# Result rows of two token tiles summed and normed among the experts, in the order of the tokens' groups

## The chip, the cores and the metric

One core of one Trainium2 chip runs the whole kernel. The metric is the time of one execution on the chip in microseconds (us), the median of several. The core's engines work side by side, each through its own list of instructions in order: TensorE (PE, matrix products), VectorE (DVE) and ScalarE (ACT, element-wise work and evictions), GpSimd (POOL), and SyncE (SP), which here only issues transfers. Transfers (DMA) are issued by SP, by ACT or by POOL and run on 16 DMA engines. An instruction that waits for a semaphore holds what stands behind it on its engine.

## The reference

One layer on 512 tokens of width 1024, in float32: attention in two branches (stick-breaking, and chunked with relative positions), gates, an output projection, a layer norm; then experts and a second layer norm. The experts are what the change is about:

```
g_sel = argmax over 4 groups of  x @ w_group + b_group            # one group per token
e     = the two best of the group's 8 experts, softmax over the two
y     = sum over the two: weight * (silu(x @ gate_e) * (x @ up_e)) @ down_e
x     = layer_norm(ALPHA * x + y) * ln2_g + ln2_b                 # x: result of the first norm
```

There are 32 experts, 1024 -> 256 -> 1024, and each token goes to two experts of one group. In the inputs used here the four groups hold 123, 132, 127 and 130 tokens, and no expert has more than 44.

## The kernel before

Up to about 400 us come the projections, the attention, the gates and the output projection, each fp32 product in three passes of split operands (`xh`, `xl`, `wh`, `wl`). Keys are evicted from a product (`pj`) in halves of 64 rows, each half written twice: into its own rows (L334, L336) and into the other head's rows (L335, L337).

Then the tokens are routed. Each expert has 64 slots, two experts are a pair, and 16 pairs make up the 32 experts. Routing leaves for every slot its token (`toki`), its weight (`wslot`) and the row that it writes (`rowi`, in `y2D`: two rows for each token, one for each of its experts). If an expert should have over 64 tokens, a flag sends all work through `dense`, behind the rest.

Each expert e runs: `gate_up(e)` (16 products `sc` of the pair's gathered rows `xp` with four weight tiles), the eviction of its two halves (`gus`: ScalarE at L1105, VectorE's add at L1106), `down(e-1)` (8 products `tr` with two weight tiles, evicted to `oe` by ScalarE and VectorE), the transposes and activation `act(e)` (`stp`, L1113, `sg`). Every other expert prepares the next pair: GpSimd gathers its rows (`fetch`, `xg`), TensorE turns them (`pj`, L1082), ScalarE and VectorE evict `xp`. After an odd expert GpSimd scatters the pair's results into `y2D` (L1147).

A weight tile `we` is 512 KB, 192 of them; SyncE loads them in the order of use (L1029: load 6e-2 to 6e+1 are gate and up of expert e from the second on, 6e+8 and 6e+9 its down part), up to 47 ahead, into four rings of buffers. At expert 20 it also loads the tokens' rows `hb` (L1299), at expert 28 the result rows `yy` (L1173), two loads for each of the four tiles of 128 tokens. The scheduler that lays out each engine's list keeps what the code pins in order, and puts transfers where it expects their buffers free.

The last two pairs (`NLATE = 2`) write no rows: their results (`late`, split in two) are added through a product with a one-hot matrix `stl`. So all four tiles are finished behind the last expert, from a list of steps (`FIN`): for each tile, products of `hb`, `yy` and `late` are collected in `fin`, then statistics, mean and gain (L1236 to L1262), and the rows go out by a plain transfer.

Of the kernel before, what the change touches and what calls it, by code (L numbers as in the profile page):

```python
# [18 lines left out]
P = 128  # L19
# [43 lines left out]
HB_AT = 20  # L63
# [12 lines left out]
Y_PE = (3,)  # L76
Y_POOL = (0, 1, 2)
F_DVE = (3,)
G_ACT = ()
FIN_TAG = ("pj", "pj", "tr", "sc", "sc", "av", "tr", "tr")  # L80
FIN_AT = {29: (0, 1, 2, 3)}
FIN = (
# [6 lines left out]
).split()  # L89
# [10 lines left out]
def trunk(ctx, tc, xT, x, wm, wv, wbr, wout, wr, br, bg, rbx, lnp, lncol, wexp, out):  # L100
# [36 lines left out]
    hD = dram.tile([S, D], F32, name="hD")  # L137

# [115 lines left out]
    ps = pp.tile([P, S], F32, tag="sc", name="warm", bufs=SCB)  # L254
    for _ in range(WARM):
        nc.tensor.matmul(ps, warm[:, :P], warm, start=True, stop=True)
# [48 lines left out]
    def proj(m_hl, evac):  # L305
        h, lo = m_hl
        ps = pp.tile([P, S], F32, tag="pj", name="pj", bufs=2)
        for c in range(C):
            mm3(ps, h[:, c * P : (c + 1) * P], lo[:, c * P : (c + 1) * P], xh[c], xl[c], c == 0, c == C - 1)
            if c % 2 == 1:  # L310
                if c == C - 1:
                    evac(ps)
                yield

    def job(kind, *a):
        if kind in ("q", "k"):
# [5 lines left out]
            def evac(ps):  # L322
                in_order[0] = (b, p) == (0, 0)

                for h in range(2):
# [14 lines left out]
            yield from proj(hl, evac)  # L340
# [230 lines left out]
    while first:  # L571
        first = [g for g in first if next(g, True) is not True]
# [73 lines left out]
    val = small([P, TT, 2], "val", at=end0)  # L646
    tokv = small([P, TT, 2], "tokv", at=end0)
# [46 lines left out]
    tok2 = keep.tile([P, 2 * NLATE], F32, name="tok2")  # L694
    flag = keep.tile([P, 1], I32, name="flag")
    xg = [keep.tile([P, D], F32, name=f"xg{k}") for k in range(XGB)]
    for t in xg:
        nc.gpsimd.memset(t, 0.0)
    onehot = keep.tile([P, TT, 4 * CAP], F32R, name="onehot")
    nc.gpsimd.memset(ones, 1.0)  # L700
# [4 lines left out]
    iota([P, TT, 2], [[2 * P, TT], [1, 2]], -2 * S, 2, "val", val)  # L705
# [145 lines left out]
    def route(tt):  # L851
# [7 lines left out]
        m = small([P, 4], f"m{tt}")  # L859
# [20 lines left out]
        mm(rk, tri, MS[:, tt, :], False, True)  # L880
        pm = small([P, 2, NE], f"pm{tt}")
# [12 lines left out]
    def finish_routing():  # L894
# [10 lines left out]

        pmf = B8[:, :2].rearrange("p q t k n -> p (q t k n)").rearrange("p (k t e) -> p k t e", k=2, t=TT)
# [20 lines left out]

        for k in range(2):
            for j in range(2):
                nc.scalar.activation(  # L930
                    tok2[j * HD : (j + 1) * HD, k * NLATE : (k + 1) * NLATE],
                    ps[k * HD : (k + 1) * HD, 1, NPAIR - NLATE :], AF.Copy, bias=1.0 * S,
                )
        nc.scalar.activation(wslot, ps[:, 2, :], AF.Copy)
# [82 lines left out]
    for e in range(NE + 1):  # L1017
        seq += [(e, c) for c in range(4) if e < NE] + [(e - 1, 4 + f) for f in range(2) if e > 0]
# [74 lines left out]
    def gate_up(e):  # L1093
# [11 lines left out]
        nc.scalar.activation(gus[e], ps[CAP:], AF.Copy)  # L1105
        nc.vector.tensor_add(gus[e], gus[e], ps[:CAP])  # L1106
# [3 lines left out]
    def act(e):  # L1110
# [41 lines left out]
    res, fs, fr, fu, parts = {}, {}, {}, {}, {}  # L1152
    stl = []
    gb2 = []
    late = []

    def last_rows():

        tok3 = bp.tile([P, 2 * NLATE], F32, tag="tok3", name="tok3", bufs=1)
        nc.vector.tensor_scalar(out=tok3, in0=tok2, scalar1=-256.0, scalar2=None, op0=OP.add)  # L1160
        for n in range(NLATE):
            st = lop.tile([P, 2, 2, 256], F32R, tag="lo", name=f"stl{n}")
            for k in range(2):
# [257 lines left out]
```

## Time and profile before

| | us |
|---|---|
| median of 3 runs (691.07 to 693.62) | 691.54 |
| the profiled execution | 692.49 |
| its span, first to last instruction | 690.8 |
| TensorE busy | 646.1 |
| VectorE, ScalarE, GpSimd busy | 400.8, 322.0, 86.9 |

The profile is of one execution, 0.95 us over the median, and 1.7 us of its time lie outside the span. Times inside it count from the span's start. "Busy" is time in which an engine has an instruction at work; a matrix product that waits for nothing still counts its pipeline. The stage table gives the busy time of each engine in one stretch; the chain of waits follows the span back from its last instruction, step by step to what released it; the timeline lists instructions in order of time, and merges neighbours of one kind (x16).

### The profile page before, as it was taken

The page shows a single profiled execution, that of the slowest core. Times are in us where ns is not written, and L with a number is a line of the kernel's source. Part 1 is how long each engine was busy: PE and PEld are TensorE (multiplying, and loading weights), DVE is VectorE, ACT ScalarE, POOL GpSimd, SP SyncE. Part 2 cuts the span into 40 slices and gives each one's busy share as a digit, 9 for nine tenths or more (in the row PEclk, how much of TensorE's full clock was granted, in tenths as well). Part 3 has the DMA queues.
Part 4 walks back from the last instruction along what each step waited for, and adds up shares of the span by engine and source line. Part 5 has one row for each costly group of instructions (what it writes and reads, how often), then busy time and mean ns, then how long its engine had stood idle before and what let it go on. Part 6 is the DMA issues. An engine that isn't in the chain of part 4 may idle for free.

```text
span 690.8 us, 8854 instructions
## 1 busy us (share of the span) xinstructions
PE 646.1 (94%) x3096; PEld 419.8 (61%) x3096; DVE 400.8 (58%) x834; ACT 322.0 (47%) x632; POOL 86.9 (13%) x134
## 2 busy tenths in 40 slices
PE   8999999899999999989999978999999988899992
PEld 4888788788878888878888764343433322223351
DVE  6776867768868887563864895233323322224347
ACT  5677877866765665745423222222322222223232
POOL 2001100101000000050000232211111111000043
PEclk9999999999999999999999999999999999999997
DMA  9600078102130322027793489999999999999923
GB/s 332 247 0 1 1 279 297 65 0 93 46 106 17 115 82 94 31 64 261 262 381 129 168 283 391 407 411 409 409 410 407 408 405 411 405 405 407 408 103 123
DMA packets 48319, 160.15 MB, mean 232 GB/s; under 512 B 7438, under 2 KB 7582, under 8 KB 48272
## 3 DMA queue, kind: packets, MB, share of 16 engines
q1 hardware_dynamic: 44208, 152.26, 57.9%
q0 software_dynamic: 4064, 7.31, 2.8%
q8 instruction: 25, 0.41, 0.2%
q14 instruction: 22, 0.18, 0.1%
HBM read 151.20 MB, written 15.73 MB: 242 GB/s over the span
## 4 chain that ended last, share of the span: by engine, by line
PE 67%; DMA 14%; DVE 12%; ACT 4%; issue 3%; SPq 0%; DVEq 0%; ACTq 0%
PE pj L126 22%; PE sc L126 13%; DMA we<-in_wexp_dram 13%; PE pv L126 6%; PE pb L126 6%; PE tr L126 6%; PE po L126 4%; PE av L126 2%; PE fin L126 2%; PE tr L523 2%; PE pj L1082 1%; DVE hp L809 1%; PE stp L1113 1%; DVE wl L111 1%; ACT wh L108 1%
## 5 line engine op out<-in xcount | busy, mean ns | idle before, releaser
L126 PE MATMUL sc<-we,xp 128*64 128x512 f32 x448 | 108.4, 604 | 3.9 <-DMA we<-in_wexp_dram 2.9
L126 PE MATMUL pj<-xh,wh 128*128 128x512 f32 x256 | 103.5, 406 | 2.4 <-DVE k L337 1.6
L126 PE MATMUL pj<-xh,wl 128*128 128x512 f32 x256 | 101.5, 396 | 0.5 <-DVE wl L111 0.5
L126 PE MATMUL pj<-xl,wh 128*128 128x512 f32 x256 | 101.5, 396 | 0.2 <-DVE xl L111 0.2
L111 DVE TENSOR_TENSOR wl<-raw,wh 128x1024 fp32r<-128x1024 f32 (+1 forms) x57 | 68.3, 1204 | 19.9 <-ACT wh L108 19.7
L1106 DVE TENSOR_TENSOR gus<-gus,sc 64x512 f32<-64x512 f32 x32 | 21.7, 679 | 97.0 <-ACT gus L1105 97.0
L126 PE MATMUL tr<-we,sg 128*64 128x512 f32 x256 | 65.0, 615 | 8.1 <-DMA we<-in_wexp_dram 6.0
L1105 ACT ACTIVATE gus<-sc 64x512 f32<-64x512 f32 x32 | 19.0, 594 | 108.5 <-PE sc L126 108.5
L108 ACT ACTIVATE wh<-raw 128x1024 fp32r<-128x1024 f32 (+1 forms) x57 | 58.7, 1038 | 19.8 <-PE pj L126 5.2
L126 PEld LDWEIGHTS sc<-we,xp 128*64 128x64 f32 x448 | 27.2, 136 | 60.2 <-issue 27.5
L126 PEld LDWEIGHTS pj<-xh,wh 128*128 128x128 f32 x256 | 49.1, 192 | 13.1 <-ACT wh L108 2.0
L126 PEld LDWEIGHTS pj<-xh,wl 128*128 128x128 f32 x256 | 48.7, 190 | 12.0 <-DVE wl L111 1.4
L126 PEld LDWEIGHTS pj<-xl,wh 128*128 128x128 f32 x256 | 49.0, 191 | 8.9 <-DVE xl L111 0.5
L126 PEld LDWEIGHTS tr<-we,sg 128*64 128x64 f32 x256 | 16.7, 138 | 49.4 <-issue 33.0
L126 PE MATMUL pb<-y,wh 128*128 128x512 f32 x128 | 40.0, 394 | 1.9 <-DVE k L337 1.9
L111 DVE TENSOR_TENSOR wl<-tr,wh 128x512 fp32r<-128x512 f32 (+1 forms) x64 | 30.7, 484 | 9.9 <-ACT wh L108 9.6
L476 POOL TENSOR_SCALAR_AFFINE_SELECT w<-w 128x128 f32<-128x128 f32 x32 | 14.6, 467 | 148.8 <-ACT w L473 146.1
L108 ACT ACTIVATE wh<-tr 128x512 fp32r<-128x512 f32 (+1 forms) x64 | 27.5, 431 | 12.0 <-PE tr L523 11.0
L126 PE MATMUL sc<-k,q 128*128 128x512 f32 (+3 forms) x128 | 29.3, 324 | 0.9 <-DVE w L472 0.9
L1147 POOL DMA_INDIRECT y2D<-oe,rowi x14 | 14.1, 1007 | 120.9 <-DVE oe L1145 93.3
L126 PEld LDWEIGHTS pb<-y,wh 128*128 128x128 f32 x128 | 23.3, 188 | 7.0 <-PE tr L523 1.6
L523 PE MATMUL tr<-ident,w 128*128 128x128 f32 x160 | 27.5, 272 | 0.0
(222 smaller groups left out, 1181.4 us busy)
## 6 DMA issues: line engine op xcount, KB each, us to landing
we<-in_wexp_dram SPq DMA_DIRECT2D x192, 512.0 KB
raw<-in_wm_dram SPq DMA_DIRECT2D x32, 512.0 KB
raw<-in_wv_dram SPq DMA_DIRECT2D x8, 512.0 KB
y2D<-zero SPq DMA_DIRECT2D x16, 256.0 KB
raw<-in_wbr_dram SPq DMA_DIRECT2D x8, 512.0 KB
raw<-in_wout_dram SPq DMA_DIRECT2D x8, 512.0 KB
yy<-y2D SPq DMA_DIRECT2D x8, 512.0 KB
strip<-in_rbx_dram SPq DMA_DIRECT2D x8, 256.0 KB
```

The costliest lines, as they stand in the source:

```text
L108: act = nc.scalar.activation(hi, src, AF.Copy)
L111: pin((eng or nc.vector).tensor_sub(lo, src, hi.bitcast(F32)), fix == "both")
L126: pin(nc.tensor.matmul(ps, a, b, start=start, stop=stop))
L476: nc.gpsimd.affine_select(out=blk, in_=blk, pattern=[[-1, P]], compare_op=OP.is_gt, fill=0.0, base=0, channel_multiplier=1)
L523: nc.tensor.transpose(tr[:, i * P : (i + 1) * P], w[:, off + j * P : off + (j + 1) * P], ident)
L809: nc.vector.scalar_tensor_tensor(out=src, in0=src, scalar=r, in1=lnb[:, cs], op0=OP.mult, op1=OP.add)
L1082: pin(nc.tensor.transpose(ps[:, c, :], xg[(p - 2) % XGB][:, o : o + P], ident))
L1105: nc.scalar.activation(gus[e], ps[CAP:], AF.Copy)
L1106: nc.vector.tensor_add(gus[e], gus[e], ps[:CAP])
L1113: pin(nc.tensor.transpose(st[:, q, :], gus[e][:, q * P : (q + 1) * P], ident[:CAP, :CAP]))
L1147: nc.gpsimd.indirect_dma_start(out=y2D[:, :], out_offset=bass.IndirectOffsetOnAxis(ap=rowi[:, p : p + 1], axis=0), in_=oe[p], in_offset=No ...
```

## The change

Tokens are given positions in the order of their groups (four counts `cg`, starts `sp`, a token's place `posi`), and `y2D` is written by position. Tile 0, the first 128 positions, has all its rows after the experts of the first two groups, tile 1 after those of the third, if these groups hold at least 128 and 256 tokens; if not, the flag of `dense` is set as well. Tiles 0 and 1 are summed and normed on VectorE at experts 24 and 29, tiles 2 and 3 behind the last expert. Tokens' own rows come by an indirect gather (`tokp`, which passes through a small table `tokD` in memory), the finished rows leave by an indirect scatter. The y loads move from SyncE to ScalarE. Expert 29's down part is computed one place later. Apart from that, 14 of the 16 copies of keys go to GpSimd, and products whose result is not used are put between products at the start and in the routing.

```diff
-HB_AT = 20
+BETWEEN = (3, 3, 1, 1)
+IDLE = {(1, 4, 4): 6, (1, 4, 5): 12}
+IDLE_LAST = 6
+K_POOL = ((0, 1), (0, 2), (0, 3), (1, 0), (1, 1), (1, 2), (1, 3))
+ROWS_AT = {22: 0, 27: 1}
+NORM_AT = {24: 0, 29: 1}
+GAIN_AT = 21
+TOKP_AT = 8
...
                         pin(nc.scalar.activation(t[r, h, 0, :], ps[r], AF.Copy))
-                        pin(nc.scalar.activation(t[o, h, 0, :], ps[r], AF.Copy))
                         pin(nc.vector.tensor_sub(t[r, h, 1, :], ps[r], t[r, h, 0, :].bitcast(F32)))
-                        pin(nc.vector.tensor_sub(t[o, h, 1, :], ps[r], t[r, h, 0, :].bitcast(F32)))
+                        if (b, p) in K_POOL:
+                            nc.gpsimd.tensor_copy(t[o, h, :, :], t[r, h, :, :])
...
+        V.tensor_scalar(out=posi, in0=p2[:, 0], scalar1=0.5, scalar2=1.0 * S, op0=OP.mult, op1=OP.add)
...
+    seq += [(e, 4 + f) for e in range(NE - 3, NE) for f in range(2)]
...
-        for tt in range(TT):
-            y2.append([slot([P, D], F32, f"yy{tt}{k}") for k in range(2)])
-            for k in range(2):
-                nc.sync.dma_start(y2[tt][k], y2v[tt, k])
...
+    def tile_rows(tt, pool):
+        for y, k, where in ((ya, 0, pool), (yb, 1, slots2)):
+            y[tt] = slot([P, D], F32, f"y{k}{tt}", where)
+            nc.scalar.dma_start(y[tt], y2v[tt, k])
+
+    def tile_res(tt):
+        hb[tt] = slot([P, D], F32, f"hb{tt}", slots2)
+        nc.gpsimd.indirect_dma_start(
+            out=hb[tt], out_offset=None, in_=hD[:, :],
+            in_offset=bass.IndirectOffsetOnAxis(ap=tokp[:, tt : tt + 1], axis=0),
+            bounds_check=S - 1, oob_is_err=False,
+        )
+
+    def tile_sum(tt, eng):
+        pin(eng.tensor_add(ya[tt], ya[tt], hb[tt]))
+        pin(eng.tensor_add(ya[tt], ya[tt], yb[tt]))
+
+    def tile_norm(tt, src, out_by):
+...
+        nc.gpsimd.indirect_dma_start(
+            out=out[:, :], out_offset=bass.IndirectOffsetOnAxis(ap=tokp[:, tt : tt + 1], axis=0),
+            in_=ya[tt], in_offset=None, bounds_check=S - 1, oob_is_err=False,
+        )
...
+        if e == NE - 1:
+            down(e - 2)
+        elif 0 < e < NE - 2:
             down(e - 1)
...
+        if e in ROWS_AT:
+            tile_res(ROWS_AT[e])
+            tile_rows(ROWS_AT[e], slots2)
+        if e in NORM_AT:
+            t = NORM_AT[e]
+            tile_sum(t, nc.vector)
+            tile_norm(t, (ya[t][:, :S], ya[t][:, S:]), "vector")
...
+    tile_sum(2, nc.vector)
+    tile_sum(3, nc.gpsimd)
...
+    tile_norm(2, fin[:2], "both")
+    tile_norm(3, fin[2:], "vector")
```

What this makes of the engines' lists shows in three places. Names in brackets are the semaphores that an instruction waits for: DMAHW0 to 7 are those of transfers issued by SP and ACT, DMASW of those by GpSimd. The first place is ScalarE at expert 23. Before, the eviction gus of expert 23 comes first, then the last part of expert 22's results and the rows of pair 12:

```order
L1105 ACTIVATE gus<-sc 64x512 [waits DVE_49,PE_49]
L1143 ACTIVATE oe<-tr,wslot 64x512 [waits DMASW6_49,PE_49,Activation_49]
L1061 ACTIVATE xp_5284<-pj 128x512 [waits PE_49]
L1115 ACTIVATE sg<-stp 128x128 [waits PE_49]
L1105 ACTIVATE gus<-sc 64x512 [waits DVE_49,PE_49]
```

The last of these rows is gus of expert 24. After the change, the list at the same place is this:

```order
L1201 ACTIVATE oe<-tr,wslot 64x512 [waits DMASW2_49,PE_49,Activation_49]
L1117 ACTIVATE xp_5409<-pj 128x512 [waits PE_49]
L1244 DMA y_5373<-y2D 128x1024 [waits DMAHW3_49,DMAHW1_49,DMAHW5_49,DMAHW0_49,DMASW4_49]
L1244 DMA y_5375<-y2D 128x1024 [waits DMAHW6_49,DMAHW4_49,DMAHW1_49]
L1164 ACTIVATE gus<-sc 64x512 [waits DVE_49]
L1174 ACTIVATE sg<-stp 128x128 [waits PE_49]
```

The last row but one is now gus of expert 23: it has moved behind oe and xp, and two transfers of result rows stand ahead of it, which wait for DMAHW5 and DMAHW6 among others.

The second place is SyncE at the loads that had these semaphores last. Before, the list is weights, then the four hb, then weights again:

```order
L1029 DMA we_5117<-in_wexp_dram 128x1024 [waits DMAHW1_49,PE_49]
L1029 DMA we_5125<-in_wexp_dram 128x1024 [waits DMAHW2_49,PE_49]
L1029 DMA we_5129<-in_wexp_dram 128x1024 [waits DMAHW3_49,PE_49]
L1299 DMA hb_5146<-hD 128x1024 [waits DMAHW4_49]
L1299 DMA hb_5148<-hD 128x1024 [waits DMAHW5_49]
L1299 DMA hb_5150<-hD 128x1024 [waits DMAHW6_49]
L1299 DMA hb_5152<-hD 128x1024 [waits DMAHW7_49]
L1029 DMA we_5155<-in_wexp_dram 128x1024 [waits DMAHW0_49]
```

After the change, the two loads number 162 and 163 (we_5137, we_5141) come first here, and the order of use is left five rows further:

```order
L1083 DMA we_5137<-in_wexp_dram 128x1024 [waits DMAHW5_49]
L1083 DMA we_5141<-in_wexp_dram 128x1024 [waits DMAHW6_49,PE_49]
L1083 DMA we_5172<-in_wexp_dram 128x1024 [waits DMAHW7_49,PE_49]
L1083 DMA we_5176<-in_wexp_dram 128x1024 [waits DMAHW0_49,PE_49]
L1083 DMA we_5180<-in_wexp_dram 128x1024 [waits DMAHW1_49]
L1083 DMA we_5214<-in_wexp_dram 128x1024 [waits DMAHW2_49]
L1083 DMA we_5235<-in_wexp_dram 128x1024 [waits DMAHW3_49]
L1083 DMA we_5336<-in_wexp_dram 128x1024 [waits DMAHW4_49]
L1083 DMA we_5378<-in_wexp_dram 128x1024 [waits DMAHW7_49,PE_49]
L1083 DMA we_5399<-in_wexp_dram 128x1024 [waits DMAHW0_49,PE_49]
```

The hb loads are gone from the queue, and six weights of later experts (we_5214 is number 170, we_5442 number 190) stand ahead of number 167.

The third place is ScalarE from expert 28 to 30. Before, the two splits of expert 28's `late` stand ahead of gus of expert 30, those of expert 29 ahead of gus of expert 31:

```order
L113 ACTIVATE late_5586<-tr,wslot 64x512 [waits DMAHW1_49,PE_49]
L1061 ACTIVATE xp_5596<-pj 128x512 [waits PE_49]
L113 ACTIVATE late_5586<-tr,wswap 64x512 [waits DVE_49]
L1115 ACTIVATE sg<-stp 128x128 [waits PE_49]
L1105 ACTIVATE gus<-sc 64x512 [waits PE_49]
L113 ACTIVATE late_5641<-tr,wswap 64x512 [waits DMAHW7_49,DMAHW2_49,PE_49]
L1115 ACTIVATE sg<-stp 128x128 [waits PE_49]
L113 ACTIVATE late_5641<-tr,wslot 64x512 [waits DVE_49]
L1105 ACTIVATE gus<-sc 64x512 [waits PE_49]
```

After the change, from gus of expert 29 to gus of expert 30, the loads of tiles 2 and 3 stand there, and the norm of tile 1:

```order
L1164 ACTIVATE gus<-sc 64x512 [waits DVE_49,PE_49]
L1244 DMA y_5721<-y2D 128x1024 [waits DMAHW7_49,DMAHW0_49,DMASW5_49]
L110 ACTIVATE late_5670<-tr,wslot 64x512 [waits PE_49]
L1117 ACTIVATE xp_5680<-pj 128x512 [waits PE_49]
L1174 ACTIVATE sg<-stp 128x128 [waits PE_49]
L1244 DMA y_5723<-y2D 128x1024 [waits DMAHW0_49,DMASW1_49]
L110 ACTIVATE late_5670<-tr,wswap 64x512 [waits DVE_49]
L1244 DMA y_5725<-y2D 128x1024 [waits DMAHW2_49,DMAHW1_49]
L1244 DMA y_5727<-y2D 128x1024 [waits DMAHW2_49]
L1268 ACT_TABLE_LOAD
L1268 ACTIVATE mv<-mv,epsf 128x1 [waits DVE_49]
L1164 ACTIVATE gus<-sc 64x512 [waits PE_49]
```

Four transfers, a table load and the norm's logarithm now stand ahead of gus of expert 30.

## Rows read from the trace of the kernel before

**Rows 1.** Stage table: stretch, length, busy PE, PEld, DVE, ACT, POOL, clock

```profile
421.00:536.00 115.00, 111.64 (x567) 42.35 (x566) 36.41 (x69) 32.24 (x67) 18.29 (x18) 0.99 1.03 409
...
536.00:655.00 119.00, 107.49 (x488) 35.43 (x486) 35.09 (x73) 28.69 (x55) 10.07 (x10) 1.00 1.02 407
```

**Rows 2.** Chain of waits, experts: start us, us, what

```profile
450.38 3.58 PE sc L126 x16
...
462.79 3.58 PE sc L126 x16
...
536.13 12.01 DMA we<-in_wexp_dram
...
649.96 0.39 PE stp L1113 x4
```

**Rows 3.** Timeline of SyncE's queue: start us, us, what, count

```profile
611.40 4.12 SPq L1299 DMA_DIRECT2D hb<-hD  x4
...
617.85 27.72 SPq L1029 DMA_DIRECT2D we<-in_wexp_dram  x22
```

**Rows 4.** Waits of SyncE's queue: us in total, times, longest

```profile
SPq L1029 <- DMA we<-in_wexp_dram: 152.5, 146, 2.3
```

**Rows 5.** Timeline of the end, all engines

```profile
657.86 1.28 ACT L1117 ACT_TABLE_LOAD   x1
...
658.83 1.94 PE L126 MATMUL tr<-we,sg 128*64 128x512 f32 x8 [1.49 <-DVE sg L1119]
...
663.02 0.75 DVE L114 SCALAR_TENSOR_TENSOR late<-tr,wslot,late 64x512 fp32r<-64x512 f32 x1 [0.75 <-ACT late L113]
...
673.23 5.31 PE L126 MATMUL fin<-yy,ident 128*128 128x512 f32 x12
...
675.85 0.69 DVE L1236 BATCH_NORM_STATS2 bsf<-fin 128x6 f32<-128x512 f32 x1
...
677.50 0.75 DVE L1254 SCALAR_TENSOR_TENSOR res<-fin,mv,gb 128x512 f32<-128x512 f32 x1
...
680.11 0.69 DVE L1236 BATCH_NORM_STATS2 bsf<-fin 128x6 f32<-128x512 f32 x1
...
684.48 1.42 DVE L1262 SCALAR_TENSOR_TENSOR res<-res,mv,gb 128x512 f32<-128x512 f32 x2
...
685.26 0.99 SPq L1266 DMA_DIRECT2D out_dram<-res  x2
```

**Rows 6.** Head of the page

```profile
span 690.8 us, 8854 instructions
```

**Rows 7.** Timeline of SyncE's queue, windows from 600 and 604.2 us

```profile
601.22 3.06 SPq L1029 DMA_DIRECT2D we<-in_wexp_dram  x3
...
603.96 6.55 SPq L1029 DMA_DIRECT2D we<-in_wexp_dram  x6
```

**Rows 8.** Timeline around expert 23

```profile
580.13 0.59 ACT L1105 ACTIVATE gus<-sc 64x512 f32<-64x512 f32 x1 [4.14 <-PE sc L126]
...
580.76 0.68 DVE L1106 TENSOR_TENSOR gus<-gus,sc 64x512 f32<-64x512 f32 x1 [3.96 <-ACT gus L1105]
...
583.45 0.58 ACT L1061 ACTIVATE xp<-pj 128x512 f32<-128x512 f32 x1
...
583.72 0.46 PE L1113 MATMUL stp<-ident,gus 64*128 64x64 f32 x4
```

**Rows 9.** Groups of instructions: page, tile k, end

```profile
L111 DVE TENSOR_TENSOR wl<-raw,wh 128x1024 fp32r<-128x1024 f32 (+1 forms) x57 | 68.3, 1204 | 19.9 <-ACT wh L108 19.7
...
L335 ACT ACTIVATE k<-pj x16: 590/595/597, 23.2 to 254.7; 64x512 fp32r<-64x512 f32 x16
...
L336 DVE TENSOR_TENSOR k<-pj,k x16: 672/688/695, 24.0 to 255.3; 64x512 fp32r<-64x512 f32 x16
...
L1214 POOL TENSOR_TENSOR yy<-yy,yy 128x1024 f32<-128x1024 f32 x3 | 7.1, 2364 | 24.8 <-DMA yy<-y2D 24.5 <-issue 0.2
```

**Rows 10.** Stage table, first half-speed stretch

```profile
10.70:14.10 3.40, 3.40 (x9) 2.63 (x10) 2.94 (x4) 2.46 (x3) 0.00 (x0) 0.50 1.03 411
```

More of the change, by code (lines that the diff above doesn't have):

```diff
@@ L253, in trunk, with idle_products @@
     nc.vector.memset(warm, 0.0)
-    ps = pp.tile([P, S], F32, tag="sc", name="warm", bufs=SCB)
-    for _ in range(WARM):
-        nc.tensor.matmul(ps, warm[:, :P], warm, start=True, stop=True)
+    warm_ps = pp.tile([P, S], F32, tag="sc", name="warm", bufs=SCB)
+    def idle_products(n):
+        for _ in range(n):
+            pin(nc.tensor.matmul(warm_ps, warm[:, :P], warm, start=True, stop=True))
+    idle_products(WARM)
     xh, xl = [], []
@@ L303, in trunk, with proj @@
     merged = []
-    def proj(m_hl, evac):
+    def proj(m_hl, evac, between=()):
         h, lo = m_hl
@@ L571, in trunk @@
     while first:
-        first = [g for g in first if next(g, True) is not True]
+        left = []
+        for g in first:
+            in_order[0] = True
+            if next(g, True) is not True:
+                left.append(g)
+        first = left
+    in_order[0] = False
     for b in range(2):
@@ L699, in trunk @@
     onehot = keep.tile([P, TT, 4 * CAP], F32R, name="onehot")
+    zr = keep.tile([P, P], F32R, name="zr")
+    nc.gpsimd.memset(zr.bitcast(F32), 0.0)
     nc.gpsimd.memset(ones, 1.0)
@@ L1047, in trunk @@
             first_x(c, [t])
+        for _ in range(IDLE.get(k, 0)):
+            mm(first[NFIRST - 1], zr, onehot[:, 1, :], False, False)
     in_order[0] = False
@@ L1086, in prep_first @@
         for c in range(C):
+            if c == 0:
+                for _ in range(IDLE_LAST):
+                    mm(first[NFIRST - 1], zr, onehot[:, 2, :], False, False)
             first_x(c, range(TT - 1, TT) if c < NFIRST else range(TT))
@@ L1186, in gain_rows @@
                 nc.scalar.activation(gb2[k][:, j * S : j * S + S], ps, AF.Copy)
-    y2, hb = [], []
-    fin, added = {}, {}
-    def fin_open(n):
-        tt, cs = n // 2, slice(n % 2 * S, n % 2 * S + S)
-        fin[n] = pb.tile([P, S], F32, tag=FIN_TAG[n], name=f"fin{n}", bufs=NBUF[FIN_TAG[n]])
-        mm(fin[n], ident, hb[tt][:, cs], True, False)
-        added[n] = 0
-    def fin_add(n, upto):
-        tt, cs = n // 2, slice(n % 2 * S, n % 2 * S + S)
-        for k in range(added[n], upto):
-            end = k == 2 * NLATE - 1 and FIN.index(f"add{n}.{k + 1}") > FIN.index(f"rows{tt}")
-            mm(fin[n], stl[k][:, tt * P : (tt + 1) * P], late[k][:, cs], False, end)
-        added[n] = upto
@@ new lines, in late_slots @@
+    def late_slots():
+        st = lop.tile([P, 2 * NLATE, 2 * P], F32R, tag="lo", name="stl")
+        for n in range(NLATE):
+            for k in range(2):
+                i = k * NLATE + n
+                one = st[:, 2 * n + k]
+                V.tensor_scalar(out=one, in0=iota256, scalar1=tok2[:, i : i + 1], scalar2=None, op0=OP.is_equal)
+                V.scalar_tensor_tensor(
+                    out=one, in0=iota256, scalar=tok3[:, i : i + 1], in1=one.bitcast(F32), op0=OP.is_equal, op1=OP.add
+                )
+                stl.append(st[:, 2 * n + k])
@@ L1282, in trunk @@
                 fetch(p)
+            for tt in range(TT):
+                nc.gpsimd.indirect_dma_start(
+                    out=tokD[:, :], out_offset=bass.IndirectOffsetOnAxis(ap=posi[:, tt : tt + 1], axis=0),
+                    in_=toks[:, tt : tt + 1], in_offset=None, bounds_check=S - 1, oob_is_err=False,
+                )
+        if e == TOKP_AT:
+            nc.scalar.dma_start(tokp, tokD.rearrange("(t p) o -> p (t o)", p=P))
         in_order[0] = True
-        for n in fin:
-            fin_add(n, len(late))
-        if e > 0:
+        if e == NE - 1:
+            down(e - 2)
+        elif 0 < e < NE - 2:
             down(e - 1)
```

221 lines of the change are left out of this document (107 added, 114 removed), and 6 rows, old and new, of the table FIN.

## The prediction

> **What bounds the kernel now.** I read the stage table first, then the chain of waits, then the queue's own waits, then the timeline around the places that the change touches. From 421 to 655 us the experts run, and the stage table shows two limits in them [rows 1]. Up to 536 TensorE is busy 111.64 of 115 us, and the chain shows a pair of experts every 12.41 us (462.79 - 450.38) [rows 2]. At 536.13 the chain leaves TensorE: it is "DMA we", piece after piece, with TensorE busy 107.49 of 119 us and the DMA engines still at 1.02 of their share [rows 1, 2]. So the second half of the experts runs at the pace of the weight loads, 27.72 us for 22 loads of 512 KB, 1.26 us each [rows 3]. The reader is to see that a weight is used about as soon as it lands. SyncE, which issues these loads, waited 146 times for an earlier load, 152.5 us in all [rows 4]: every transfer issued by an engine takes one of eight semaphores in turn (DMAHW0 to 7 in the orders shown with the change) and first waits for the transfer that had it before. At most eight are under way, and the wait is served by the engine that issues. The end is a chain of another kind: the last expert product ends at 660.77 [rows 5], the span at 690.8 [rows 6], 30.0 us of sums and norms for four tiles.
>
> **The change, part by part.** The forecast hangs on one move. Before, the eight loads of result rows (yy) come last on SyncE's queue. Now they stand on ScalarE's queue, which also evicts every expert's products, and they are spread from expert 22 to 29. ScalarE takes its instructions in order, so a load that waits holds the evictions behind it.
>
> Step 1, the first stop. The order of ScalarE shows y_5373 and y_5375 (tile 0) behind oe and xp_5409 and ahead of the eviction gus of expert 23. Their semaphores (DMAHW5 and 6) were last given to we_5137 and we_5141, which the order of SyncE shows as the loads number 162 and 163. Expert 23 itself uses loads up to 139, and its neighbour's down part 140 and 141. When is load 163 there? In the trace the last 22 loads stand behind hb, so the six issued from 603.96 are 164 to 169, and the three from 601.22 are 162, 163, 164 [rows 3, 7]. Eight transfers further is the second hb, at about 612.7 (611.40 and a third of 4.12) [rows 3]; its issue says that 163 has landed. The DMA engines are full, so the new kernel can't have it sooner by more than the hb loads it drops, which come later; it adds two gathers of 512 KB (hb, tiles 0 and 1) ahead of it, 2 x 1.26. That gives 615.2. ScalarE is at this point at 584.03 (xp, 583.45 + 0.58) [rows 8]. So it stands for some 31 us, with gus behind it, and behind gus VectorE's add, TensorE's transposes stp of expert 23 and every later expert. TensorE goes on at 615.2 + 0.59 + 0.68 = 616.5, where it stood at 583.72 before [rows 8]: 32.8 us late.
>
> Step 2, what is won back. In the stop the loads ran on until the buffers were full, so experts 24 to 27 run at TensorE's pace, two pairs, 24.8 us, and not at the loads' pace. Ahead of gus of expert 25, VectorE has the sum and norm of tile 0: two adds of 1.20 [rows 9], two statistics, four gains of 0.75 and the small ones, some 7.5 us. About 3.5 of it lies beside expert 25's products (3.58) [rows 2], 4 are on the path. So gus of expert 27 is done at about 645.5. Right behind it comes the next stop: tile 1's first load waits for load 179, 24 transfers after 163 (19 weights in SyncE's new order, two y loads, two scatters, one out): 615.2 + 24 x 1.26 = 645.4. These two meet; from here loads and ScalarE go hand in hand.
>
> Step 3, the last load. The eighth y load (y_5727) waits for load 188. Behind 163 and up to it stand 26 weights (25, and number 190, which the new order pulls ahead), seven y loads, two hb gathers, three y2D scatters and one out scatter: 39 x 1.26 = 49.1, so R = 664.3. The nearest lower bound is TensorE's own pace to this place, 645.5 and a pair and a half, 660 to 664.
>
> Step 4, from R to the last product. Behind y_5727 stand a table load, Ln, gus of expert 30, a second table load and Exp, and on VectorE the rest of tile 1's norm ahead of the add. A norm takes 4.26 a tile (680.11 - 675.85) [rows 5], of which the statistics, 1.4, are done; with the table loads (2 x 1.28) [rows 5], gus (0.59 + 0.68) [rows 8] and two gains that ran on other engines (2 x 0.75) [rows 5] it is 8.2. From stp of expert 30 to the end of the last product the old kernel needs 10.8 (649.96 to 660.77) [rows 2, 5]; the new one holds expert 29's down part back into this stretch, 1.9 more. Last product at R + 20.9 = 685.2, where it was 660.8.
>
> Step 5, the new end. The splits of the last expert take 3.0 behind the products (663.02 + 0.75 - 660.77) [rows 5]. Then VectorE adds tile 2's rows, 2 x 1.20, and TensorE takes four products on sums, 1.8 (5.31 for 12) [rows 5]: R + 28.1. Norm of tile 2, 4.26; norm of tile 3 from statistics to its last row, 5.8 as before (680.11 to 685.9) [rows 5]: R + 38.2. The issue by GpSimd and the landing take what the old end took from its last issue, 690.8 - 686.2 = 4.6, and 1.0 for the indirect issue: R + 43.8. The second scatter waits for the first; I add 1.2, with 0 and 4.6 (once more the same landing) as bounds. The span ends at R + 45 = 709.3. So the end is 24.1 us after the last product where it was 30.0: two tiles fewer bring 5.9, as meant, against 24 lost.
>
> Step 6, the early edits. Fourteen second halves of k move from ScalarE (0.59) and VectorE (0.69) [rows 9] to one GpSimd copy each. No row shows such a copy. If it takes what an add of 128x1024 takes, 2.36 [rows 9], each k is 1.1 later than today, 14 x 1.1 = 15 at worst; if it is hidden, the freed engines may give back up to the 3.5 us that TensorE waits there. The products put in to keep TensorE busy can at best turn a half-speed stretch of 3.4 us (granted clock 0.50, so 1.2 GHz, busy 3.40) [rows 10] into one at 2.4 GHz, 1.7, and there are two such, at the start and in the routing; they cost what they run. The routing gains some 13 small VectorE operations and four tokD scatters ahead of the first gathers, 2 to 3 us. I take 0 for all, nearest to a TensorE that is busy nearly without a gap in the attention, and keep -5 to +15.
>
> Sum: the span goes from 690.8 to 709.3 [rows 6]. The profiled execution took 692.49, 1.7 more than its span, and the median of the runs is 691.54, 0.95 less than that execution. So 709.3 + 1.7 - 0.95 = 710.
>
> A rule speaks against step 1. The Trainium skill, "DMA: Bandwidth & Descriptors", section "Issuing engines are not separate DMA queues", says that transfers started by ScalarE, SyncE or GpSimd share the same 16 engines, and that the choice of engine saves only the issuing time. By it alone the y loads are as cheap on ScalarE as on SyncE, and rival A's 686 follows. The section "Anatomy of one DMA" of the same page adds that a semaphore wait is served on the issuing sequencer before dispatch; SyncE's 146 waits [rows 4] agree with that one.
>
> **The rivals.** A: ScalarE isn't held, because the loads are far enough ahead when it gets there. Then the last product stays at about 661 and the end shrinks to 24.1 us: span 685, time 686, faster. For it speaks that in the first half of the experts loads are ahead of TensorE; against it that at 575 to 602 TensorE waits for single weights, so that load 163, of expert 27, can't be there at 584. B: only the first stop counts; later y loads find their semaphores free, and TensorE runs freely. Then four pairs after 616.5 bring stp of expert 31 to 666.1, last product 3.9 later, 24.1 for the end: span 694, time 695, slower by 0.5%. Against it: no row has transfers faster than 1.26, and TensorE at 1.03 a load (12.41 for 12) overtakes them. C: the GpSimd copies of k hold the attention, +15 on the forecast, 725: slower still. For it, every score product waits for k; against it, half of k is ready for the other head as before. D: some of the stop is hidden, or the early edits and the shorter end together pay for B: 690 to 693, no change. That the change doesn't do what it says would need a group count that sends all tokens through the dense branch; the inputs' groups hold 123, 132, 127 and 130 tokens and no expert over 64, which doesn't.
>
> **How the numbers follow.** Forecast 0.60, B 0.15, C 0.10, A 0.10, D 0.05. About 0.5% (3.5 us) is what a measurement of this kernel can tell from no change. Faster by more: 0.09 (A, but for its upper edge). Within: 0.06 (D and that edge). Slower: 0.85. The forecast's own range is 703 to 717 (R by 4, the last scatter by 3, early edits by 5). The range that leaves out no more than two in ten reaches to B below and nearly to C above: 695 to 722.
>
> **What would show it right or wrong.** Step 1: a gap on ScalarE of some 30 us ahead of gus of expert 23, released by a DMA, and TensorE idle for as long, with the DMA share falling when the buffers are full. Step 2: no waits for weights in the pairs after it. Step 3: further gaps on ScalarE at the y loads of tiles 1 to 3. Step 4: the last down product near 685. Step 5: some 24 us after it. Wrong is the forecast if ScalarE's longest gap after 575 is under 10 us; then A or D holds. If TensorE's waits before 400 us grow by over 5 us, C does.

## The result: slower by 6.6%, and the profile after

The changed kernel takes 738.69 us (median of four runs, 735.51 to 740.61), the kernel before 692.58 in the same session: a ratio of 1.066, interval 1.063 to 1.069. Slower, as forecast, but by 46 us where 18.5 were forecast, and outside the range. The profiled execution has 46.1 us more span than before [rows 6]; this is the head of its page and the two groups in which the new waits show (after the bar: busy time, mean ns, idle time before them and what ended it).

```profile
span 736.9 us, 8852 instructions
...
L1164 ACT ACTIVATE gus<-sc 64x512 f32<-64x512 f32 x32 | 19.0, 593 | 132.2 <-PE sc L123 104.3
...
L1172 PE MATMUL stp<-ident,gus 64*128 64x64 f32 x128 | 15.6, 246 | 43.9 <-DVE gus L1165 43.9
```

Of ScalarE's 132.2 us ahead of gus, 104.3 are waits for products, as before (108.5 there); the other 27.9 are one wait. TensorE's 43.9 us ahead of stp are four waits, the longest 29.5.

The stage table of after answers to [rows 1] (same columns: stretch, length, busy time of PE, PEld, DVE, ACT, POOL, granted clock, DMA share, GB/s).

```profile
421.00:480.00 59.00, 36.85 (x173) 13.58 (x170) 12.96 (x43) 11.58 (x26) 10.08 (x10) 0.83 0.86 277
480.00:536.00 56.00, 56.00 (x290) 21.42 (x292) 18.72 (x32) 16.08 (x32) 9.05 (x9) 1.00 1.03 410
536.00:575.00 39.00, 39.00 (x202) 14.86 (x200) 13.46 (x23) 11.04 (x23) 6.73 (x7) 1.00 1.03 409
575.00:615.00 40.00, 23.03 (x120) 10.49 (x116) 11.20 (x31) 7.14 (x13) 5.32 (x6) 0.85 1.03 409
615.00:655.00 40.00, 19.78 (x82) 7.31 (x84) 12.48 (x22) 8.81 (x14) 3.04 (x2) 0.68 1.00 395
655.00:691.00 36.00, 30.12 (x138) 10.94 (x134) 13.03 (x21) 9.29 (x18) 4.00 (x4) 0.91 0.69 245
```

Two holes stand in it. The second, 575 to 655, is the forecast one. The first, 421 to 480, is not: TensorE is busy 36.85 us, the DMA engines move 277 GB/s, and before, the same stretch read so:

```profile
421.00:480.00 59.00, 55.64 (x281) 21.05 (x279) 18.00 (x38) 16.23 (x35) 9.18 (x9) 0.97 1.03 410
```

GpSimd's timeline of after shows what stands in the first hole: the four scatters of token numbers (tokD), each behind the one before (in brackets: idle time, and what ended it). Only the first is issued ahead of the first gathers (432.34 to 435.00).

```profile
430.18 1.07 POOL L1306 DMA_INDIRECT tokD<-toks,posi  x1 [14.81 <-DVE small_oe L964]
438.69 1.02 POOL L1306 DMA_INDIRECT tokD<-toks,posi  x1 [2.69 <-DMA tokD<-toks,posi]
449.07 0.99 POOL L1306 DMA_INDIRECT tokD<-toks,posi  x1 [9.36 <-DMA tokD<-toks,posi]
458.12 0.96 POOL L1306 DMA_INDIRECT tokD<-toks,posi  x1 [6.79 <-DMA tokD<-toks,posi]
```

ScalarE's timeline of after shows both holes as waits in its own queue (ACTq is its sequencer, here issuing a DMA):

```profile
464.18 0.39 ACTq L1311 DMA_DIRECT2D tokp<-tokD  x1
464.63 0.68 ACT L1201 ACTIVATE oe<-tr,wslot 64x512 f32<-64x512 f32 x1 [19.03 <-DMA tokD<-toks,posi]
...
599.58 0.58 ACT L1117 ACTIVATE xp<-pj 128x512 f32<-128x512 f32 x1
626.41 1.58 ACTq L1244 DMA_DIRECT2D y<-y2D  x2
628.04 0.59 ACT L1164 ACTIVATE gus<-sc 64x512 f32<-64x512 f32 x1 [27.88 <-DMA we<-in_wexp_dram]
...
685.61 0.81 ACTq L1244 DMA_DIRECT2D y<-y2D  x2
```

The load of tokp reads what the fourth scatter writes, and an eviction oe of an early expert stands behind it for 19.03 us (the code asks for this load at expert 8; on ScalarE's list it stands ahead of expert 4). At 600.16 ScalarE stands again, until the first two y loads get their semaphores at 626.41. In the first stop the DMA share falls to 0.51 and 0.45 (449 to 458 and 458 to 464 us), so most loads stand too; in the second it stays at 1.03 (600 to 626.4), so the loads run on for its whole length. TensorE's timeline shows what each stop costs there, and what follows it:

```profile
465.84 5.70 PE L123 MATMUL sc<-we,xp 128*64 128x512 f32 x16 [17.76 <-ACT xp L1117]
...
629.40 0.69 PE L1172 MATMUL stp<-ident,gus 64*128 64x64 f32 x4 [29.48 <-DVE gus L1165]
630.02 5.53 PE L123 MATMUL sc<-we,xp 128*64 128x512 f32 x16
...
637.58 3.65 PE L123 MATMUL sc<-we,xp 128*64 128x512 f32 x16
...
649.80 0.69 PE L1172 MATMUL stp<-ident,gus 64*128 64x64 f32 x4 [5.82 <-DVE gus L1165]
...
697.21 0.69 PE L1172 MATMUL stp<-ident,gus 64*128 64x64 f32 x4 [7.17 <-DVE gus L1165]
...
709.26 1.94 PE L123 MATMUL tr<-we,sg 128*64 128x512 f32 x8
```

The sixteen products sc after a stop take 5.53 us, the next sixteen 3.65. The granted clock was 0.50 (1.2 GHz) in the idle stretch from 615 to 629 us, 0.50 still from 629.4 to 632.5, and 1.00 from 635.5 to 641: the group behind this stop begins at the lower level and ends at the higher. Over the groups behind the other stops it was 0.56 to 0.64. The last product ends at 711.2, the span 25.7 us later (30.0 before); the issue of the last out scatter, 4.10 us behind the one before, closes it:

```profile
732.13 0.97 POOL L1284 DMA_INDIRECT out_dram<-y,tokp  x1 [3.12 <-DVEq L1362]
```

### The profile page after: what moved, and what is told of

Its sections match the earlier page's. It is cut to its first block, busy times and chain, and to the rows that moved or that the text cites. A ratio compares the mean times of both kernels' runs of the same rounds, so it can differ in the third digit from the quotient of the medians.

```text
span 736.9 us, 8852 instructions
## 1 busy us (share of the span) xinstructions
PE 636.3 (86%) x3084; PEld 420.3 (57%) x3084; DVE 405.1 (55%) x850; ACT 317.9 (43%) x624; POOL 110.0 (15%) x158
## 4 chain that ended last, share of the span: by engine, by line
PE 51%; DVE 17%; DMA 14%; issue 8%; ACT 7%; POOL 2%; SPq 0%; ACTq 0%; POOLq 0%; DVEq 0%
PE pj L123 14%; PE sc L123 13%; DMA we<-in_wexp_dram 7%; PE pb L123 6%; PE tr L123 4%; PE po L123 4%; DVE t L476 2%; DVE wl L108 2%; PE pv L123 2%; DMA tokD<-toks,posi 2%; PE av L123 2%; ACT wh L105 2%; DMA raw<-in_wm_dram 1%; DVE t L474 1%; PE tr L530 1%
## 5 line engine op out<-in xcount | busy, mean ns | idle before, releaser
L123 PE MATMUL sc<-we,xp 128*64 128x512 f32 x448 | 113.2, 651 | 22.5 <-ACT xp L1117 22.5
L108 DVE TENSOR_TENSOR wl<-raw,wh 128x1024 fp32r<-128x1024 f32 (+1 forms) x57 | 69.9, 1231 | 23.0 <-ACT wh L105 22.9
L123 PEld LDWEIGHTS sc<-we,xp 128*64 128x64 f32 x448 | 32.0, 149 | 81.1 <-issue 47.5
L1164 ACT ACTIVATE gus<-sc 64x512 f32<-64x512 f32 x32 | 19.0, 593 | 132.2 <-PE sc L123 104.3
L123 PE MATMUL tr<-we,sg 128*64 128x512 f32 x256 | 61.9, 604 | 0.4 <-DMA we<-in_wexp_dram 0.3
L123 PEld LDWEIGHTS pj<-xh,wl 128*128 128x128 f32 x256 | 48.1, 188 | 11.6 <-DVE wl L108 1.3
L1172 PE MATMUL stp<-ident,gus 64*128 64x64 f32 x128 | 15.6, 246 | 43.9 <-DVE gus L1165 43.9
L1172 PEld LDWEIGHTS stp<-ident,gus 64*128 64x128 f32 x128 | 11.0, 147 | 61.5 <-DVE gus L1165 57.9
L483 POOL TENSOR_SCALAR_AFFINE_SELECT w<-w 128x128 f32<-128x128 f32 x32 | 16.1, 514 | 125.0 <-ACT w L480 123.0
L1203 DVE TENSOR_SCALAR oe<-tr,wswap 64x512 f32<-64x512 f32 x14 | 10.6, 755 | 38.5 <-ACT oe L1201 38.4
```

The costliest lines, as they stand in the source:

```text
L108: pin((eng or nc.vector).tensor_sub(lo, src, hi.bitcast(F32)), fix == "both")
L123: pin(nc.tensor.matmul(ps, a, b, start=start, stop=stop))
L483: nc.gpsimd.affine_select(out=blk, in_=blk, pattern=[[-1, P]], compare_op=OP.is_gt, fill=0.0, base=0, channel_multiplier=1)
L1164: pin(nc.scalar.activation(gus[e], ps[CAP:], AF.Copy))
L1172: pin(nc.tensor.transpose(st[:, q, :], gus[e][:, q * P : (q + 1) * P], ident[:CAP, :CAP]))
L1203: nc.vector.tensor_scalar(out=oe[p][sides[odd], cs], in0=ps[here], scalar1=sc, scalar2=None, op0=OP.mult)
```

## The experiments

The ratios are to the kernel before, run beside each, with 95% intervals; the medians of before were 691.96, 692.02 and 692.03 us in the three sessions. Rows come from one profiled execution of each kernel; where it stands well off the median, its time is given.

**The tokp load off ScalarE.**

```
-  nc.scalar.dma_start(tokp, tokD...)
+  nc.gpsimd.dma_start(tokp, tokD...)
```

> The changed kernel with one edit: the load of the small table tokp is issued by GpSimd instead of ScalarE. Theory M (two stops of ScalarE that add up): ScalarE's idle time of 19 us behind expert 3, which ended with the last tokD scatter, goes, TensorE's 17.8 us there too, and the stream of weights no longer loses its 19 us; the second stop at tile 0's loads stays near 28 us but lies some 19 us earlier: 738.7 - 19 = 719 to 721. Rival (the later stop swallows the earlier, since the stream sets it): the first gap goes and the second grows by as much, 735 to 739.

Measured: 732.36 us, 1.061 (1.056 to 1.065). That lies between the two expectations. The long stop on ScalarE is gone, yet only 6.3 us come back. The stage table of this kernel says why: the weights still come slowly.

```profile
421.00:480.00 59.00, 48.76 (x242) 19.01 (x238) 16.95 (x49) 14.21 (x31) 11.98 (x12) 0.92 1.02 326
```

The DMA engines read as fully busy (1.02) and move 326 GB/s where 410 were moved before. So the first hole has two parts: the stop, and transfers slowed while the scatters are under way. The y stop stays (ScalarE 27.22 us, TensorE 28.81).

**The y loads on SyncE.** The edit above, and:

```
-  nc.scalar.dma_start(y[tt], y2v[tt, k])
+  nc.sync.dma_start(y[tt], y2v[tt, k])
```

> The changed kernel with tokp's load on GpSimd and the eight y loads on SyncE, where the old kernel had them. Theory M (a y load waits for its turn behind weights of much later experts, whoever issues it): ScalarE no longer stops, but y loads of tile 0 stand behind load 180 on SyncE, and VectorE, whose sum of tile 0 stands ahead of expert 25's add, waits for them; the stop moves from ScalarE to VectorE and is no shorter: 710 to 720. Rival (only the hold of ScalarE by its own queue costs): both stops go, 684 to 692.

Measured: 739.45 us, 1.068 (1.062 to 1.075), no better than the change itself and above the expected 710 to 720. ScalarE is free, but VectorE now takes its place. Its timeline and TensorE's in this kernel:

```profile
650.27 1.23 DVE L1255 TENSOR_TENSOR y<-y,hb 128x1024 f32<-128x1024 f32 x1 [32.46 <-DMA y<-y2D]
```

```profile
660.34 0.69 PE L1172 MATMUL stp<-ident,gus 64*128 64x64 f32 x4 [43.80 <-DVE gus L1165]
```

On SyncE the first two y loads stand behind weights of later experts: it issues 19 of these from 615.69, where TensorE is about to stop, and the y loads at 640.01. VectorE, in order, waits with tile 0's first sum ahead of gus of a later expert. The stop is not ScalarE's: it goes wherever the first instruction in order meets the late rows.

**The y loads on GpSimd.** As the last, with `nc.gpsimd` for both.

> The changed kernel with tokp's load and the eight y loads on GpSimd, whose transfers take semaphores of their own, so that no y load waits for the landing of a weight of a later expert. Theory M: the long gaps on ScalarE and VectorE ahead of gus of experts 23 and 25 go; what stays is the shorter end (24 to 26 us behind the last product, where the old kernel has 30) and the y loads' place in the stream, up to 5 us later last weights: 684 to 692. Rival (the norm among the experts, its table loads and gus behind it, is what costs): 700 to 715, with gaps of over 10 us left at the two norms.

Measured: 707.01 us, 1.023 (1.019 to 1.028): 25.4 below the first experiment, by the eight y loads' issuer alone. GpSimd evicts no products, and behind its waits TensorE waits for no gathered rows (none of its waits after 575 us is for xp). TensorE's longest wait is now 11.36 us, at tile 0's norm (625.68). The expected 684 to 692 isn't reached, the first hole being still there. The time lies in the rival's range (700 to 715), and the wait at the norm is of the size that it names; two later kernels, without rows and without norms, test it.

**The early edits alone.** The kernel before with the copies of k on GpSimd, the extra products, and nothing of the tokens' order.

```
+  if (b, p) in K_POOL:
+      nc.gpsimd.tensor_copy(t[o, h, :, :], t[r, h, :, :])
...
+  idle_products(between[c])
...
+  mm(first[NFIRST - 1], zr, onehot[:, 1, :], False, False)   # IDLE times
```

> The old kernel with the early edits alone: 14 copies of keys on GpSimd, and the products whose result is not used at the start and in the routing. Theory M: the first expert starts about 3 us earlier (418.3 against 421.5 us in the profiles) and this reaches the end in part, since weights bound the second half: 688 to 691.5. Rival (the copies on GpSimd hold the scores): 694 to 706.

Measured: 688.48 us (ten runs), 0.995 (0.993 to 0.997), 3.5 us under before and clear of the noise. Its group of copies, and TensorE's last product:

```profile
L347 POOL CAST k<-k 64x1024 fp32r<-64x1024 f32 x14 | 14.5, 1037 | 65.7 <-DVE k L345 65.6
```

```profile
654.93 1.94 PE L130 MATMUL tr<-we,sg 128*64 128x512 f32 x8 [1.49 <-DVE sg L1145]
```

A copy takes 1.04 us, not 2.36, and holds no attention. The whole program moves forward by some 4 us (last product 656.87, before 660.77), and the end behind it stays at 30.1.

**tokp without DRAM.** The change, with the token of each place computed by one-hot products on TensorE; no scatters, no load.

```
-  nc.gpsimd.indirect_dma_start(out=tokD[:, :], ...)   # x4
...
-  nc.scalar.dma_start(tokp, tokD...)
...
+  V.tensor_scalar(out=onehot[:, tt, :], in0=iota256, scalar1=posf[...], ..., op0=OP.is_equal)
...
+  mm(ps[:, 2 * k + q, :], onehot[:, tt, q*P:(q+1)*P], toks[:, tt, :], tt == 0, tt == TT - 1)
```

> The changed kernel without the table in memory: the token of each position (tokp) comes from one-hot products on TensorE at expert 8, so the four tokD scatters and the load of tokp are gone; the y loads stay on ScalarE. Theory S (the scatters of 4-byte rows slow every other transfer while they are under way: 326 GB/s where 409 is usual over 59 us, which is 12 us of stream; moving tokp's load alone gave 6 because the loss stayed): 738.7 less the hold of ScalarE and the lost stream, 717 to 722. Rival H (the hold of ScalarE was all, and e1 has taken it out): 730 to 734.

Measured: 721.67 us, 1.041 (1.038 to 1.044): 17.0 below the change, so 10.7 beyond the first experiment. The first hole is filled, in this kernel's stage table:

```profile
421.00:480.00 59.00, 54.40 (x276) 21.14 (x272) 20.64 (x60) 16.38 (x35) 9.19 (x9) 0.97 1.03 409
```

And this is the kernel that the forecast had reckoned with. Its ScalarE, and the groups sc behind TensorE's four longest stops (the profiled execution took 724.2 us):

```profile
610.41 1.53 ACTq L1246 DMA_DIRECT2D y<-y2D  x2
611.99 0.59 ACT L1166 ACTIVATE gus<-sc 64x512 f32<-64x512 f32 x1 [25.90 <-DMA we<-in_wexp_dram]
...
652.42 0.68 ACT L1203 ACTIVATE oe<-tr,wslot 64x512 f32<-64x512 f32 x1 [5.42 <-DMA y2D<-oe,rowi]
```

```profile
613.96 6.02 PE L123 MATMUL sc<-we,xp 128*64 128x512 f32 x16
...
634.85 5.82 PE L123 MATMUL sc<-we,xp 128*64 128x512 f32 x16
...
653.64 6.66 PE L123 MATMUL sc<-we,xp 128*64 128x512 f32 x16 [4.14 <-ACT xp L1119]
...
682.54 5.87 PE L123 MATMUL sc<-we,xp 128*64 128x512 f32 x16
...
694.09 1.94 PE L123 MATMUL tr<-we,sg 128*64 128x512 f32 x8
```

The stop begins at 586.1 and ends at 612.0; the forecast had 584 and 615.2.

**The same, y loads on GpSimd too.**

> As the kernel before this one, with the eight y loads on GpSimd. Theory S: 707.0 of the kernel with the scatters, less 12 us of stream: 693 to 697. Rival H (the rate of the stream fell for another reason, such as more weights in the wrong order): 703 to 708.

Measured: 694.08 us (ten runs, 692.34 to 701.91), 1.0045 (1.001 to 1.008). The y loads' issuer is worth 27.6 us here. With both causes gone the change still doesn't gain. TensorE's two longest waits in the profiled execution, one of the longer ones (699.31 us):

```profile
618.70 0.69 PE L1174 MATMUL stp<-ident,gus 64*128 64x64 f32 x4 [12.78 <-DVE gus L1167]
...
655.16 1.97 PE L123 MATMUL sc<-we,xp 128*64 128x512 f32 x4 [5.98 <-DMA we<-in_wexp_dram]
```

The first is VectorE's sum and norm of tile 0, ahead of gus in its order: they begin at 607.31, gus at 617.97, and of these 10.7 us only 1.35 are a wait for rows. The second is a weight. The last product ends at 671.55 and the span, 697.3, is 25.8 later.

**Four idle scatters in the kernel before.** They write numbers that nothing reads.

```
+  nc.gpsimd.indirect_dma_start(out=tokD[:, :], out_offset=...(ap=toks[:, tt : tt + 1]), in_=toks[...], ...)   # x4
```

> The old kernel with the four scatters of 128 four-byte rows added at the place where the change has them (behind the first gathers on GpSimd), their result not used by anything. Theory S: the stream of weights, which bounds the second half, loses 10 to 13 us and the kernel with it: 701 to 705. Rival H: 2 KB in all are nothing, 690 to 694; at most the next gathers come late on GpSimd's queue, 694 to 697.

Measured: 703.58 us, 1.017 (1.012 to 1.021). They were placed elsewhere than meant, from 307.85 to 344.40 in the output projection, so this doesn't reproduce the place, and that the time falls into 701 to 705 is luck. It does show that the scatters cost: the stage table of this kernel,

```profile
340.00:360.00 20.00, 11.05 (x39) 8.72 (x40) 11.65 (x26) 8.28 (x20) 0.98 (x1) 0.74 0.88 170
```

and of the kernel before:

```profile
340.00:360.00 20.00, 20.00 (x94) 16.25 (x93) 15.01 (x35) 7.38 (x24) 0.00 (x0) 1.00 0.99 372
```

**Norms earlier.** As the kernel of 694.08, with `ROWS_AT = {22: 0, 25: 1}` and `NORM_AT = {24: 0, 27: 1}`.

> The kernel with tokp from TensorE and y loads on GpSimd, and tile 1's rows fetched at expert 25 and normed at expert 27 instead of 27 and 29. Theory N (a norm ahead of an expert's add stops TensorE for some 11 us; early enough, the weights that land meanwhile are caught up, since an expert takes TensorE 6.2 us and the stream 8.3): 2 to 5 us under the kernel with tile 1 at 29: 689 to 694. Rival (the end is set by the stream's last load anyway, and the y loads move ahead of weights): the same time within 1 us.

Measured: 696.53 us, 1.006 (1.004 to 1.009). Nothing comes back: the time is 2.5 us over 694.08, outside both expectations; the wait at tile 0's norm is 11.36 us.

**Gains earlier in the kernel of the early edits.** `gain_rows()` at expert 21 in place of 28.

> The old kernel with the early edits, and the rows of gain (32 transposes, four evictions) made at expert 21 instead of 28. Theory G (at expert 28 TensorE is close to bounding again, and these 8 us of small products lie on the path to the last product): 684 to 687.5, the last product 1 to 3 us earlier than at 656.8 of the run without it. Rival (the last weight's landing at 655 sets the end): 688 to 689, no change against the early edits alone.

Measured: 689.71 us (twelve runs), 0.996 (0.994 to 0.998): no gain over 688.48.

**No rows for tiles 0 and 1.** As the kernel of 694.08, without their four y loads and sums.

```
-  tile_rows(ROWS_AT[e], slots2)
+  ya[ROWS_AT[e]] = hb[ROWS_AT[e]]
...
-  tile_sum(t, nc.vector)
```

> The kernel with tokp from TensorE and y loads on GpSimd (694.1), without the y loads of tiles 0 and 1 and their two sums: their rows are normed without the experts' part, so four transfers of 512 KB and four adds of 1.2 us are left out. Theory T (what is left of the loss against the early edits alone, 5.6 us, is that these rows travel ahead of the last weights, 4 x 1.26): 688 to 690. Rival Q (the norms among the experts, which hold gus and TensorE for 11 us each, are the loss): 692 to 694.

Measured: 688.64 us (twelve runs), 0.9965 (0.995 to 0.998), 5.4 less than with them. Four transfers of 1.26 us are 5.0. The sums went with the loads, so the two aren't apart. TensorE still stops for 13.22 us at tile 0's norm, so this stop, the rival's cause, is not what the 5.4 us were. Its last product:

```profile
658.40 1.94 PE L123 MATMUL tr<-we,sg 128*64 128x512 f32 x8
```

**No norms for tiles 0 and 1.** As the kernel of 694.08, with the sums scattered as they are.

> The same kernel of 694.1 with the norms of tiles 0 and 1 left out: their rows are loaded, summed and scattered, not normed. Theory T: 692 to 694. Rival Q: 686 to 690, with TensorE's stop of 12.8 us ahead of expert 25's transposes down to 3 to 5 us.

Measured: 701.5 us (six runs, three of 696.73 to 698.07 and three of 704.92 to 705.24, so that the median stands between), 1.012 (1.008 to 1.017): where neither theory had more than 694. In the profiled execution (704.92 us) TensorE's wait shrinks from 12.78 to 5.44 us, and another grows:

```profile
610.33 0.66 PE L1174 MATMUL stp<-ident,gus 64*128 64x64 f32 x4 [5.44 <-DVE gus L1167]
...
660.95 1.97 PE L123 MATMUL sc<-we,xp 128*64 128x512 f32 x4 [9.45 <-DMA we<-in_wexp_dram]
```

The y loads of tiles 2 and 3 are issued at 645.66 here and at 655.08 with the norms, and SyncE's last weight load at 658.8, there at 654.1: 4.7 us later, where four transfers of 1.26 us are 5.0. So the freed time seems to go to y loads that pass the last weights. That reading fits the rows, but no run tests it.

**The idle scatters where the change has them.** The kernel before, with an index that comes out of the routing.

```
+  V.tensor_scalar(out=posz, in0=ps[:, 0, :TT], scalar1=0.0, ..., op0=OP.mult)
+  V.tensor_add(posi, posz, tokg)
```

> The old kernel with the four scatters of 4-byte rows behind the routing, where the change has them (in the earlier run the scheduler had put them at 308 us, into the output projection). Their result is not used. Theory S: the stream moves 250 to 330 GB/s for some 40 us behind the routing, and the kernel loses 9 to 13 us: 701 to 705. Rival H (in the earlier run the loss came from the weights of the output projection being late, not from the scatters' load on the transfers): 692 to 695.

Measured: 712.59 us, 1.029 (1.027 to 1.032): 20.6 us for 2 KB that nobody reads, above both expectations. Its stage table, and ScalarE:

```profile
421.00:480.00 59.00, 42.12 (x205) 16.21 (x206) 14.06 (x34) 12.37 (x29) 11.12 (x11) 0.85 1.06 296
480.00:536.00 56.00, 56.00 (x284) 21.15 (x282) 17.89 (x30) 15.91 (x31) 8.11 (x8) 0.98 0.99 373
```

```profile
475.68 0.68 ACT L1152 ACTIVATE oe<-tr,wslot 64x512 f32<-64x512 f32 x1 [14.79 <-DMA y2D<-oe,rowi]
```

With no tokp load on ScalarE, an eviction still waits 14.79 us, for a scatter of result rows that GpSimd issues behind the third of these scatters (462.64). The loss itself is in the transfers, which are busy all the while (1.06 and 0.99) but move 296 and 373 GB/s where before moved 410 and 409. As an estimate that is 59 x (1 - 296/410) + 56 x (1 - 373/409) = 21.3 us of transfers lost, beside the 20.6 measured.

**Where the time is.** In medians: the change 738.7; tokp's load off ScalarE 732.4 (-6.3); the scatters away 721.7 (-10.7); the y loads on GpSimd 694.1 (-27.6); the rows of tiles 0 and 1 not fetched or summed 688.6 (-5.4), what the early edits alone give (688.5). The first two steps agree with an estimate of what the transfers lost from 421 to 480 us, 59 x (1 - GB/s / 410): 19.1 us in the change, 12.1 without tokp's load on ScalarE, 0.1 without the scatters. The last equality hides two things that cancel: the kernel without these rows has the shorter end (25.7 us behind its last product, 30.1 with the early edits alone), but its last product ends 3.5 us later (660.34 against 656.87). The fastest kernel run is the one with the early edits alone, 0.5% under before.

## Why the prediction was right and wrong, by its steps

**Step 1 was right**, mechanism and size. With the first hole taken away the stop is 25.90 us at 586.1 (forecast 31 at 584); in the change it is 27.88 from 600.16, moved 14 us later by what came before. The issuer of the y loads is its cause: nothing else was edited between 721.67 and 694.08. That edit changes two things at once, what stands behind the wait and which transfers' semaphores are waited for, and no run parts them; with the loads on SyncE, which frees ScalarE but leaves them late, the stop went to VectorE. One sign didn't come: the DMA share did not fall in this stop (1.03).

**Step 6 failed**, with "four tokD scatters ahead of the first gathers, 2 to 3 us". Nothing of before showed a scatter of four-byte rows, and the working gave it no bounds of its own, as it gave the copies, and took it at 0 in the sum; 2 to 3 us have room for issues (1.0 us each) and none for four landings, one behind the other. It also missed that the tokp load stands on ScalarE's queue behind the last of them; step 1's own reasoning, used on that load, would have found it. Taking both out, with products on TensorE in their place, brought 17.0 us. By the Trainium skill, "DMA: Bandwidth & Descriptors", section "Anatomy of one DMA — SWDGE (gpsimd) path", a transfer takes some 2 us plus its bytes by the bandwidth, so four in a row would be 8, an estimate. Here each took 8.3 (median) to land, and the measurement decides. The copies and the extra products, taken as 0 in -5 to +15, are -3.5.

**The clock was no term at all.** Of the 27.6 us between the forecast's span (709.3) and the measured one, 14.6 go with the scatters and the tokp load (736.9 - 722.3, profiled executions). The other 13.0 lie in the kernel without scatters: 6.8 up to the last y load, 4.0 from there to the last product, 2.2 behind it. Four of its groups sc, one behind each of the longest stops, take 6.02, 5.82, 6.66 and 5.87 us where 3.65 is usual, at a granted clock of 0.54 to 0.61: 9.8 us, 7.6 of them before the last y load. TensorE waits for no weight after 613 us there, so this time is not hidden behind the loads. The forecast priced the waits and let TensorE go on at full speed behind them.

**Steps 2 and 3.** The pairs after the first stop wait for no weights, as said; the norm of tile 0 holds TensorE 5.82 us (forecast 4). Step 3's mechanism didn't come. The forecast has loads and ScalarE go hand in hand from the second stop on, so that load 188 sets R. In the kernel without scatters SyncE has issued its last weight by 647.6, and R is 671.1 (forecast 664.3), set by the engines. Its second stop (5.42 us on ScalarE, 4.14 on TensorE) ends with a scatter of result rows, issued 7.8 us before the y load, and not with load 179. R in the change is 686.4.

**Step 4.** From R to the last product: 20.9 forecast, 24.8 measured, 2.1 of it the low clock behind the norm of tile 1.

**Step 5.** The end is 25.7 us after the last product, forecast 24.1. So the two tiles bring 4.3 us where 5.9 were reckoned. But the work has gone into a stretch that the transfers fill: in the kernel of 694.08 the four y loads of tiles 0 and 1 come ahead of the last weights, 5.0 us, and removing those loads and sums gave 5.4 back. Even without them the shorter end doesn't show beside the early edits alone, since the last product ends 3.5 us later; what makes these 3.5 no run takes apart.

**Rivals.** A (the loads are ahead) is refuted by the stop. The Trainium skill, "DMA: Bandwidth & Descriptors", section "Issuing engines are not separate DMA queues", says that transfers run on the same DMA engines whoever started them. The rows agree with that (407 GB/s from 575 to 615 us with ScalarE as the issuer, 405 with GpSimd). But rival A's reading, that the issuer is then indifferent, fails: its choice was worth 27.6 us, by what stands behind the wait and by what is waited for. The y loads on SyncE cost the most, 739.45 us against 732.36 on ScalarE and 707.01 on GpSimd. B has the later y loads nearly right (in the kernel without scatters only one more of them holds ScalarE for long, 5.42 us), but it fails by that stop, by those at the norms and by the low clock. C (the copies hold the attention) is refuted by the early edits alone. D's thought that early edits and end could pay for a stop fell with its size.

**Open**: why 701.5 us without the norms of tiles 0 and 1, and what makes the last product 3.5 us later when the rows of tiles 0 and 1 are left out; and whether their y loads, issued after the last weight, would let the shorter end show.

## What to carry to other kernels

A DMA on a compute engine's queue costs what stands behind its wait, not its issue: before placing one, find which transfer its semaphore last belonged to and when that lands, for every load the edit adds, the small ones too. A stage that was bound by transfers gave nothing back here for work moved into it with transfers of its own, so count them against the last weight. And price a scatter by its landing and by what the other transfers lose meanwhile, not by its bytes.

## What the runs showed of the hardware

A scatter of 128 rows of four bytes took 8.3 us to land in the change (median, 6.0 to 10.1), and 11.6 and 11.1 in the two kernels with idle scatters. Over the stretch from 421 to 480 us, in which they were under way, all transfers together moved 326 and 296 GB/s (the first and the last experiment) at a DMA share of 1.02 and 1.06, where 410 are usual; in the last, from 449 to 460 us, with the second scatter under way, 228 GB/s at 1.00. The two kernels with idle scatters differ by 9.0 us (703.58 and 712.59), and by where these stand.

Behind TensorE's stops in the change and in the kernel without scatters (4.14 to 29.48 us), the next group of sixteen products began at the lower of the two levels of the granted clock: 5.5 to 6.7 us in place of 3.65, 1.9 to 3.0 us a stop.
